# An HGRN2 / gated-MLP step on one core: how the first stage interleaves the f and q products of head 0

## The chip, the core and the metric

The kernel runs on one core of a Trainium2 chip. What is measured is the device time of one launch, in microseconds (us). Three runs of the kernel before took 1850.86, 1850.94 and 1852.46 us, median 1850.94.

A core has five engines that run their own instruction streams beside each other: PE (TensorE, matrix products; its weight loads are listed apart as PEld), DVE (VectorE), ACT (ScalarE), POOL (GpSimd) and SP (SyncE, which here issues the transfers). Each works its stream in order and waits on semaphores for what the others produce.

## The reference

The program is one step of a two-layer decoder trunk for 1024 prompt rows and 8 sample rows. Only its beginning matters here:

```python
h = x
hn = rmsnorm(h, norm_mix[0])                 # mean of squares over D_MODEL = 1024
proj = hn @ w_in                             # hgrn2_mixer
q, f, i, z = jnp.split(proj, [D_MODEL, 2 * D_MODEL, 2 * D_MODEL + D_INNER], axis=-1)
q = jax.nn.silu(q)                           # 8 heads of 128
logf = logaddexp(log(lbh), log1p(-lbh) + log_sigmoid(f));  k = -expm1(logf)
...
h = h + y
gate = jax.nn.sigmoid(rmsnorm(h, norm_ple[0]) @ w_ple_gate[0])
h = h + gate * (p[0] @ w_ple_proj[0])        # p: 256 columns a row
```

All is computed in fp32.

## The kernel before

**Layout.** Activations lie transposed: 128 partitions hold 128 features, the rows of the batch run along the columns. The 1032 rows are cut into three chunks of 384, 384 and 264 columns (`W`), and 1024 features are eight tiles, k = 0 to 7 (`KT`).

**A product in three parts.** An fp32 product is made of three passes: `mm3` (L228 to L230) multiplies high part by high part (L228), the low part of the activation by the high part of the weight (L229), and the high part of the activation by the low part of the weight (L230). A high part is a rounded copy made by ACT; a low part is what is left, a subtraction. For weights the pair is `whi` (ACT, L149) and `wlo` (DVE, L150), 128x1024 at a time; for activations it is made by `split` (L222 to L224): `bh` by ACT, `bl` by the engine handed in. One `ps_proj` tile of an output block takes 8 x 3 products.

**Who sets the order.** PE's stream is in the order of the code (a manual schedule). On the other engines a list scheduler orders instructions by priority: code position, moved forward by `tc.high_priority(offset=PRI)`; `tc.issue_after(x)` puts an instruction behind another. The code is written as generators that `Ticks` advances: a process that yields n goes on n ticks later. So tables of small numbers say how many ticks lie between the steps of a norm, and with them where a norm's two pieces of PE work stand in PE's stream: `SQD` (ticks ahead of a chunk's squares), and `SDEL[c]` (ticks from the squares to the sum, and from the sum to the broadcast).

**The first stage, in order.** Twelve products of zeros warm PE up (L113 to L118). The weights of the first p projection are loaded (`load(0)`), then p of chunks 0 and 1 (`load_p`), then x. `pple` (L339) makes twelve blocks of p's products, four for each chunk, and stores them for later. Beside them run three processes `first_norm(c)` (L579). Each squares its chunk's eight tiles on ACT and adds them in pairs (chunk 0 on DVE, the others on POOL), so four tiles remain. `norm_sum` (L266) sums over features with one-column products on PE (`pss`, L279) and raises to -1/2 on POOL; `norm_bc` (L285) broadcasts the result to all partitions by products with the identity (`pbc`, L290). Then `norm_proc` (L293) scales tile by tile on DVE (`xs`, L303, in place) and splits: `bh` on ACT (L223), `bl` on POOL for even tiles and on DVE for odd ones (L224). The same `norm_proc` serves the two later norms that precede the per-layer gate.

Then come head 0's products, chunk by chunk: `fk` (L600) makes f with 24 products, reads the sum with two sigmoids and two scalings on ACT (L606 to L609); `qq` (L614) makes q with 24 more, one sigmoid and a multiplication on DVE (L620). The f weight is `take("a", 8)`, the q weight `take("a", 0)`; `take` also starts the split of the next weight in line. The norm of a later chunk runs while the products of the chunk ahead of it run, and its sum and broadcast stand between them: chunk 1's both inside chunk 0's products, chunk 2's broadcast between f and q of chunk 1. After chunk 2's q the z products of head 0 follow (two blocks m over three chunks), and beside them `mix_x` forms sums and differences of the normed x on DVE (L426 to L429) for the rest of z.

## Time and profile before

| | |
|---|---|
| three runs, median (lowest to highest) | 1850.94 us (1850.86 to 1852.46) |
| the profiled execution's own time | 1854.45 us |
| its span (first to last instruction) | 1852.4 us |
| busy in the span: PE / DVE / ACT / POOL | 1817.2 / 1364.2 / 896.1 / 403.7 us |
| instructions of PE / DVE / ACT / POOL | 14458 / 2760 / 1905 / 407 |

The profile is of one execution, 3.5 us longer than the median of the three runs. A row of the timeline reads: start, length, engine, line, operation, output<-inputs with their shapes, how many such instructions in a row stand in this row (x4), and in brackets the engine's idle time ahead of it with what ended it. A row with a count gives the time from the start of its first instruction to the end of its last. Durations overlap where an engine pipelines, so the spacing of starts is the cost of one in a row of many.

The table by stretches gives, for each stretch of the span, its length and, for PE, PEld, DVE, ACT and POOL in that order, the busy time and the number of instructions, then the granted TensorE clock (1.00 is full), and the DMA engines' share and rate. Lines of the kind `PE out L229 <- DVE bl L224: a, n, b` are waits: an engine and line, what it waited for, the total wait, how many, and the longest.

### The profile page before, as it was taken

How to read it: one execution, taken by the hardware profiler on the slowest of the kernel's cores; microseconds unless marked ns; L12 is line 12 of the kernel's file. 1: busy time of each engine (PE TensorE's matmuls, PEld its weight loads, DVE VectorE, ACT ScalarE, POOL GpSimd, SP SyncE). 2: the span in 40 equal slices, each digit the busy share in tenths (PEclk: the TensorE clock that was granted, in tenths of full speed). 3: DMA queues.
4: the chain of work that ended last, by engine and by line, in shares of the span. 5: the costliest groups of instructions: out<-in, count | busy, mean ns of one | idle time of the engine just before them, and what ended most of it. 6: DMA issues, size and time to landing. Idle time of an engine off the chain costs nothing.

```text
span 1852.4 us, 37136 instructions
## 1 busy us (share of the span) xinstructions
PE 1817.2 (98%) x14458; PEld 1784.3 (96%) x14458; DVE 1364.2 (74%) x2760; ACT 896.1 (48%) x1905; POOL 403.7 (22%) x407
## 2 busy tenths in 40 slices
PE   8999999999999999999999999999999999999997
PEld 7999999999999999999999999999999998999997
DVE  7766788889788886877746755577778877877744
ACT  7533366556656656454435544433343345445442
POOL 4000011111011110000324233354444551000222
PEclk9999999999999999999999999999999999999999
DMA  6233343346444357863144433323334546953223
GB/s 222 79 111 104 116 128 119 118 142 190 143 136 135 113 170 223 273 206 105 57 163 137 123 106 91 102 84 124 123 101 148 177 124 223 295 190 98 69 92 115
DMA packets 164561, 258.11 MB, mean 139 GB/s; under 512 B 16097, under 2 KB 136865, under 8 KB 163361
## 3 DMA queue, kind: packets, MB, share of 16 engines
q1 hardware_dynamic: 164384, 255.74, 43.6%
q8 instruction: 113, 1.85, 0.4%
q14 instruction: 64, 0.52, 0.1%
HBM read 182.88 MB, written 72.80 MB: 138 GB/s over the span
## 4 chain that ended last, share of the span: by engine, by line
PE 81%; DVE 10%; DMA 5%; issue 2%; POOL 1%; ACT 1%; SPq 0%; DVEq 0%; POOLq 0%; ACTq 0%
PE ps_proj L228 19%; PE ps_proj L230 19%; PE ps_proj L229 19%; PE ps_d L228 3%; PE ps_d L230 3%; PE ps_d L229 3%; PE ps_o L228 2%; PE ps_o L230 2%; PE ps_o L229 2%; DMA vb<-vd 1%; PE psp L1528 1%; DVE wlo L150 1%; PE pt_o L901 1%; PE pt_g L1410 1%; DVE bl L224 1%
## 5 line engine op out<-in xcount | busy, mean ns | idle before, releaser
L228 PE MATMUL ps_proj<-bh,whi 128*128 128x264 f32 (+1 forms) x2248 | 719.3, 320 | 4.8 <-ACT u L494 1.6
L229 PE MATMUL ps_proj<-bl,whi 128*128 128x264 f32 (+1 forms) x2248 | 700.9, 312 | 5.3 <-DVE bl L224 2.7
L230 PE MATMUL ps_proj<-bh,wlo 128*128 128x264 f32 (+1 forms) x2248 | 700.9, 312 | 1.2 <-DVE wlo L150 1.2
L228 PEld LDWEIGHTS ps_proj<-bh,whi 128*128 128x128 f32 x2248 | 423.4, 188 | 12.8 <-PE pt_k L873 3.5
L229 PEld LDWEIGHTS ps_proj<-bl,whi 128*128 128x128 f32 x2248 | 423.9, 189 | 8.8 <-DVE bl L224 5.5
L230 PEld LDWEIGHTS ps_proj<-bh,wlo 128*128 128x128 f32 x2248 | 422.4, 188 | 2.1 <-DVE wlo L150 2.1
L150 DVE TENSOR_TENSOR wlo<-wstg,whi 128x1024 fp32r<-128x1024 f32 x148 | 186.7, 1261 | 110.1 <-ACT whi L149 109.8
L149 ACT CAST whi<-wstg 128x1024 fp32r<-128x1024 f32 x148 | 155.3, 1049 | 147.5 <-PE ps_proj L229 124.6
L149 ACT CAST shi<-ssum 128x512 fp32r<-128x512 f32 x152 | 94.0, 622 | 190.3 <-PE ps_proj L229 90.7
L150 DVE TENSOR_TENSOR slo<-ssum,shi 128x512 fp32r<-128x512 f32 x152 | 113.7, 751 | 9.4 <-ACT shi L149 8.9
L237 POOL TENSOR_TENSOR rsq<-rms_e,mhalf 128x3 f32<-128x3 f32 x15 | 17.8, 1187 | 359.7 <-DVE rms_e L282 359.7
L859 DVE TENSOR_TENSOR qk<-qk,t 128x384 f32<-128x384 f32 (+1 forms) x144 | 77.4, 541 | 11.9 <-PE pC L809 11.1
L228 PE MATMUL ps_proj<-xmh,shi 128*128 128x384 f32 x244 | 83.1, 340 | 0.5 <-DVE u L498 0.3
L230 PE MATMUL ps_proj<-xmh,slo 128*128 128x384 f32 x244 | 81.8, 335 | 0.0
L229 PE MATMUL ps_proj<-xml,shi 128*128 128x384 f32 x244 | 81.7, 335 | 0.0
L228 PE MATMUL ps_o<-bh,whi 128*128 128x384 f32 (+1 forms) x232 | 73.5, 317 | 0.0
L230 PE MATMUL ps_o<-bh,wlo 128*128 128x384 f32 (+1 forms) x232 | 72.8, 314 | 0.0
L229 PE MATMUL ps_o<-bl,whi 128*128 128x384 f32 (+1 forms) x232 | 72.7, 314 | 0.0
L1537 POOL TENSOR_TENSOR s<-s,u 128x384 f32<-128x384 f32 (+1 forms) x48 | 54.1, 1127 | 71.2 <-DVE s L1531 70.6
L1276 DVE TENSOR_TENSOR tmp<-tmp,pj 128x384 f32<-128x384 f32 (+1 forms) x48 | 25.6, 534 | 55.9 <-ACT tmp L1275 52.1
L237 POOL TENSOR_TENSOR rsq<-ss_e,mhalf 128x3 f32<-128x3 f32 (+2 forms) x32 | 28.7, 896 | 143.2 <-DVE ss_e L895 143.2
L264 POOL TENSOR_TENSOR ssq<-ssq,tmp 128x384 f32<-128x384 f32 (+1 forms) x36 | 34.2, 951 | 108.0 <-ACT tmp L263 108.0
(376 smaller groups left out, 4134.1 us busy)
## 6 DMA issues: line engine op xcount, KB each, us to landing
wstg<-in_wina SPq DMA_DIRECT2D x48, 512.0 KB, 3.7
wstg<-in_winb SPq DMA_DIRECT2D x48, 512.0 KB, 4.2
pj<-ppd SPq DMA_DIRECT2D x16, 516.0 KB, 4.5
S<-in_st SPq DMA_DIRECT2D x16, 512.0 KB, 5.6
vb<-vd SPq DMA_DIRECT2D x16, 512.0 KB, 4.9
out_so_s<-S SPq DMA_DIRECT2D x16, 512.0 KB, 3.5
wstg<-in_wouta SPq DMA_DIRECT2D x16, 512.0 KB, 4.1
wstg<-in_wgate SPq DMA_DIRECT2D x16, 512.0 KB, 3.7
```

Of the source, the lines that this page charges most:

```text
L149: A.copy(hi, src)
L150: V.tensor_tensor(lo, src, hi.bitcast(F32), ALU.subtract)
L224: last["lo"] = eng.tensor_tensor(lo, src, hi.bitcast(F32), ALU.subtract)
L228: PE.matmul(ps, wh, xh, start=first, stop=False, skip_group_check=more)
L229: PE.matmul(ps, wh, xl, start=False, stop=False, skip_group_check=more)
L230: PE.matmul(ps, wl, xh, start=False, stop=last, skip_group_check=more)
L237: G.tensor_tensor(y, e, mhalf[:, :n], ALU.pow)
L264: eng.tensor_tensor(ssq, ssq, sq[:, :w], ALU.add)
L859: V.tensor_tensor(lev, lev, t2.rearrange("p two (n o) -> p two n o", o=1).broadcast_to([P, 2, n, lv]), ALU.mult)
L901: PE.transpose(pt[:, m, :], on[:, m * P:(m + 1) * P], ident)
L1276: V.tensor_tensor(gt[:, :w], gt[:, :w], pj[:, OFF[c]:OFF[c] + w], ALU.mult)
L1537: G.tensor_tensor(s[:, :w], s[:, :w], us[mm, c][:, :w], ALU.mult)
```

## The change

It edits the code of the first stage and the functions that this stage calls (`load_p`, `pple`, `norm_proc`).

- **Warm-up.** The zeros are 128 columns wide; each of the twelve products reads one of them, broadcast to 512 columns.
- **Loads.** The first weight goes, as two pieces of 256 and 768 columns, through `load_split` into tiles that belong to chunk 2's activations (`hh[2]`, `hl[2]`, free so early). The transfers are issued as: first piece, p of chunk 0 (two halves, by `load_p(..., single=True)`), second piece, p of chunk 1, x of chunk 0. Two further weights are fetched ahead of x of chunk 1. Chunk 0's p is split in two halves, the weight in two pieces.
- **Order on PE.** `proj2` makes f and q of chunks 0 and 1 together: three products for f, then three for q, for each k, with a tick behind each of the first six. Chunk 2 has f, then q, as before. So there are more ticks in a chunk, and `SQD` and `SDEL` have other numbers.
- **Norms.** In the first norms all low parts are made by DVE, the scaling of tile j waits in the order until the low part of tile j-2 has been issued, and both have a raised priority. In chunks 1 and 2 the squares are not added in pairs, so `norm_sum` sums eight tiles instead of four.
- **ACT.** The copies that read out the first half of p's products have a raised priority. A sigmoid of a scrap tile (`gone`) follows the preparation of lb, which brings the table load forward; the squares of chunk 2 stand behind the last split of chunk 1, not its fourth.
- **Later norms.** `norm_proc` sets `high_priority(offset=0)` around the scaling and the split of every other norm. There nothing is raised, but the instructions of DVE and ACT come out in another order.

The diff, cut to its core:

```diff
-SQD = (0, 6, 12)
+SQD = (0, 11, 17)
 KB = 1
-SDEL = ((6, 3), (6, 2), (4, 2))
+SDEL = ((8, 2), (7, 2), (8, 2))
...
-        zf = zp.tile([P, 512], F32, name="zf")
+        zf = zp.tile([P, P], F32, name="zf")
         V.memset(zf, 0.0)
-        zr = zp.tile([P, 512], F32R, name="zr")
+        zr = zp.tile([P, P], F32R, name="zr")
         V.tensor_copy(zr, zf)
         zo = zps.tile([P, 512], F32, name="zo")
         for _ in range(NWARM):
-            PE.matmul(zo, zr[:, :P], zr, start=True, stop=True)
+            PE.matmul(zo, zr, zr[:, 0:1].broadcast_to([P, 512]), start=True, stop=True)
...
+        lows = []
         for j in range(KT):
             t = src(j) if own else sp.tile([P, 384], F32, name="tmp", bufs=4)
-            V.scalar_tensor_tensor(t[:, :w], src(j), g32[:, gi, j:j + 1], pbc[:, :w], ALU.mult, ALU.mult)
-            split(hh[:, j, :], hl[:, j, :], t[:, :w], V if j % 2 else G)
+            with tc.high_priority(offset=PRI if own else 0):
+                with tc.issue_after(lows[j - 2].ins) if own and j > 1 else ExitStack():
+                    V.scalar_tensor_tensor(t[:, :w], src(j), g32[:, gi, j:j + 1], pbc[:, :w], ALU.mult, ALU.mult)
+                split(hh[:, j, :], hl[:, j, :], t[:, :w], V if j % 2 or own else G)
+            lows.append(last["lo"])
...
-    def load_p(ap, l, c, ph, pl, behind=None, to=None):
+    def load_p(ap, l, c, ph, pl, behind=None, to=None, single=False):
         stg = ap.tile([P, 2, W[c]], F32, name=f"pstg{c}", bufs=1)
+        if single:
+            ph[c], pl[c] = [ap.tile([P, 2, W[c]], F32R, name=f"p{x}{c}") for x in "hl"]
+            for k in range(2):
+                load_split(ph[c][:, k], pl[c][:, k], pT[l][:, k, OFF[c]:OFF[c] + W[c]], stg[:, k])
+            return
...
-                with tc.high_priority(offset=PRI if l else 0):
+                with tc.high_priority(offset=0 if half and not l else PRI):
...
-    load(0)
+    loaded[0] = [t.rearrange("p k t -> p (k t)")[:, :1024] for t in (hh[2], hl[2])]
+    w0stg = wp.tile([P, 1024], F32, name="wstg")
+
+    def first_weights(a, b):
+        load_split(loaded[0][0][:, a:b], loaded[0][1][:, a:b], wproj[0, 0][:, a:b], w0stg[:, a:b])
+
     ph, pl = [None] * 3, [None] * 3
-    load_p(sp, 0, 0, ph, pl)
+    first_weights(0, 2 * P)
+    load_p(sp, 0, 0, ph, pl, single=True)
+    first_weights(2 * P, 1024)
     load_p(sp, 0, 1, ph, pl)
...
+    fetch_weights(1)
+    fetch_weights(2)
     load_x(1)
-    fetch_weights(1)
     load_x(2)
-    fetch_weights(2)
...
-        eng = V if c == 0 else G
         for j in range(0, KT, 2):
 
-            with tc.issue_after(last["pple" if c == 1 else "split4"].ins) if c else ExitStack():
+            with tc.issue_after(last["pple" if c == 1 else "split"].ins) if c else ExitStack():
                 A.activation(sq[:, j:j + 2, :], xs[c][:, j:j + 2, :], AF.Square)
-            eng.tensor_tensor(sq[:, j, :], sq[:, j, :], sq[:, j + 1, :], ALU.add)
-        yield from norm_proc(sp, [sq[:, j, :] for j in range(0, KT, 2)], lambda j: xs[c][:, j, :], 0, hh[c], hl[c], c, SDEL[c], True)
+        yield from norm_proc(sp, [sq[:, j, :] for j in range(0, KT, 1 if c else 2)], lambda j: xs[c][:, j, :], 0, hh[c], hl[c], c, SDEL[c], True)
...
+    gone = sp.tile([P, NH], F32, name="gone")
...
+    A.activation(gone, lb[:, 3, :], AF.Sigmoid)
+
+    def proj2(w1, w2, c):
+
+        both = [(wt, pp.tile([P, 512], F32, name="ps_proj", tag="mm", bufs=3)) for wt in (w1, w2)]
+        for k in range(KT):
+            for (wh, wl), ps in both:
+                mm3(ps[:, :W[c]], blk(wh, k), blk(wl, k), hh[c][:, k, :], hl[c][:, k, :], k == 0, k == KT - 1)
+            if k < KT - 2:
+                tk.tick()
+        return [ps for _, ps in both]
...
-        if i == 8:
-            with tc.issue_after(last["pple"].ins):
-                load(1)
+        if i == 5:
+            load(2)
         tk.tick()
     r0 = new_head()
-    wf, wq = take("a", 8), take("a", 0)
+    wf, wq = take("a", 8), loaded[2]
     for c in CH:
-        fk(0, r0, wf, c)
-        qq(0, r0, wq, c)
+        pf, pq = proj2(wf, wq, c) if c < 2 else (None, None)
+        fk(0, r0, wf, c, pf)
+        if c == 2:
+            take("a", 0)
+        qq(0, r0, wq, c, pq)
```

Three places show what that makes of the streams. In the names a number behind the underscore tells buffers apart; "x2" is two alike in a row.

The first is PE's stream at chunk 2's broadcast (`pbc`). Before, it stood between f and q of chunk 1: ahead of it products with the f weight (`whi_218`), behind it 24 products of the same chunk (`bh1`) with the q weight (`whi_494`).

```order
L228 MATMUL ps_proj_644<-bh1_137,whi_218 128x384
L229 MATMUL ps_proj_644<-bl1_140,whi_218 128x384
L230 MATMUL ps_proj_644<-bh1_137,wlo_219 128x384
L290 MATMUL pbc_675<-ident_68,rsq3_642 128x128 x2
L290 MATMUL pbc_675<-ident_68,rsq3_642 128x8
L228 MATMUL ps_proj_703<-bh1_137,whi_494 128x384
L229 MATMUL ps_proj_703<-bl1_140,whi_494 128x384
L230 MATMUL ps_proj_703<-bh1_137,wlo_495 128x384
```

Now f (`whi_224`) and q (`whi_288`) of chunk 1 alternate ahead of it, and behind it come at once the products of chunk 2 (`bh2`, `bl2`), which are made from this broadcast.

```order
L228 MATMUL ps_proj_631<-bh1_137,whi_224 128x384
L229 MATMUL ps_proj_631<-bl1_140,whi_224 128x384
L230 MATMUL ps_proj_631<-bh1_137,wlo_225 128x384
L228 MATMUL ps_proj_632<-bh1_137,whi_288 128x384
L229 MATMUL ps_proj_632<-bl1_140,whi_288 128x384
L230 MATMUL ps_proj_632<-bh1_137,wlo_289 128x384
L290 MATMUL pbc_788<-ident_68,rsq3_762 128x128 x2
L290 MATMUL pbc_788<-ident_68,rsq3_762 128x8
L228 MATMUL ps_proj_819<-bh2_138,whi_224 128x264
L229 MATMUL ps_proj_819<-bl2_141,whi_224 128x264
L230 MATMUL ps_proj_819<-bh2_138,wlo_225 128x264
```

So the 24 products of q that lay between the broadcast and the first product that needs it lie there no more.

The second place is DVE's stream behind chunk 0's broadcast. Before, five scalings came first, then the f weight's low part, and DVE's four low parts lay among the rest; the other four were POOL's.

```order
L303 SCALAR_TENSOR_TENSOR xs0_154<-xs0_154,g32_72,pbc_374 128x384 x5
L150 TENSOR_TENSOR wlo_219<-wstg_194,whi_218 128x1024
L282 TENSOR_SCALAR rms_e_481<-pss_432 128x3
L224 TENSOR_TENSOR bl0_139<-xs0_154,bh0_136 128x384 x2
L303 SCALAR_TENSOR_TENSOR xs0_154<-xs0_154,g32_72,pbc_374 128x384 x3
L224 TENSOR_TENSOR bl0_139<-xs0_154,bh0_136 128x384 x2
L150 TENSOR_TENSOR wlo_495<-wstg_200,whi_494 128x1024
```

Now scalings and low parts alternate, all eight of each on DVE, and the low parts of both weights (`wlo_225` of f, `wlo_289` of q) stand among them.

```order
L306 SCALAR_TENSOR_TENSOR xs0_154<-xs0_154,g32_72,pbc_385 128x384 x2
L150 TENSOR_TENSOR wlo_225<-wstg_194,whi_224 128x1024
L224 TENSOR_TENSOR bl0_139<-xs0_154,bh0_136 128x384
L306 SCALAR_TENSOR_TENSOR xs0_154<-xs0_154,g32_72,pbc_385 128x384
L224 TENSOR_TENSOR bl0_139<-xs0_154,bh0_136 128x384
L306 SCALAR_TENSOR_TENSOR xs0_154<-xs0_154,g32_72,pbc_385 128x384
L150 TENSOR_TENSOR wlo_289<-wstg_196,whi_288 128x1024
L224 TENSOR_TENSOR bl0_139<-xs0_154,bh0_136 128x384
L306 SCALAR_TENSOR_TENSOR xs0_154<-xs0_154,g32_72,pbc_385 128x384
L224 TENSOR_TENSOR bl0_139<-xs0_154,bh0_136 128x384
```

DVE's first low part moved from behind seven instructions to behind three, the q weight's from the end of the chunk to its middle.

The third place is DVE's stream behind chunk 2's broadcast, after the change alone (before, five scalings of 264 columns stood in a row, and POOL made half of the low parts). L648 is chunk 1's multiplication for q.

```order
L306 SCALAR_TENSOR_TENSOR xs2_156<-xs2_156,g32_72,pbc_788 128x264 x2
L648 TENSOR_TENSOR qk_783<-ps_proj_632,sg_816 128x384
L224 TENSOR_TENSOR bl2_141<-xs2_156,bh2_138 128x264
L306 SCALAR_TENSOR_TENSOR xs2_156<-xs2_156,g32_72,pbc_788 128x264
L224 TENSOR_TENSOR bl2_141<-xs2_156,bh2_138 128x264
L306 SCALAR_TENSOR_TENSOR xs2_156<-xs2_156,g32_72,pbc_788 128x264
L224 TENSOR_TENSOR bl2_141<-xs2_156,bh2_138 128x264
```

The pairs go on like this to the eighth low part, ahead of which stands one of the sums for z (L438). So each low part but the last stands behind one more scaling than the low part ahead of it, and the multiplication ahead of them all.

More of the change, by code (lines that the diff above doesn't have):

```diff
@@ L582, in first_norm @@
         sq = sp.tile([P, KT, 384], F32, name="sq0", bufs=2)[:, :, :W[c]]
-        eng = V if c == 0 else G
         for j in range(0, KT, 2):
-            with tc.issue_after(last["pple" if c == 1 else "split4"].ins) if c else ExitStack():
+            with tc.issue_after(last["pple" if c == 1 else "split"].ins) if c else ExitStack():
                 A.activation(sq[:, j:j + 2, :], xs[c][:, j:j + 2, :], AF.Square)
-            eng.tensor_tensor(sq[:, j, :], sq[:, j, :], sq[:, j + 1, :], ALU.add)
-        yield from norm_proc(sp, [sq[:, j, :] for j in range(0, KT, 2)], lambda j: xs[c][:, j, :], 0, hh[c], hl[c], c, SDEL[c], True)
+            if not c:
+                V.tensor_tensor(sq[:, j, :], sq[:, j, :], sq[:, j + 1, :], ALU.add)
+        yield from norm_proc(sp, [sq[:, j, :] for j in range(0, KT, 1 if c else 2)], lambda j: xs[c][:, j, :], 0, hh[c], hl[c], c, SDEL[c], True)
+    gone = sp.tile([P, NH], F32, name="gone")
     V.tensor_tensor(lb[:, 1, :], lb[:, 0, :], lb[:, 0, :], ALU.subtract)
@@ L597, in trunk_kernel, with fk @@
     V.tensor_scalar(lb[:, 3, :], lb[:, 2, :], -1.0, 1.0, ALU.mult, ALU.add)
-    def fk(h, r, wt, c):
+    A.activation(gone, lb[:, 3, :], AF.Sigmoid)
[7 more added lines that the diff above has]
+        return [ps for _, ps in both]
+    def fk(h, r, wt, c, ps=None):
         w = W[c]
-        ps = proj(wt, hh[c], hl[c], c)
+        ps = ps or proj(wt, hh[c], hl[c], c)
         f = fq.tile([P, 384], F32, name="f", bufs=3)
@@ L612, in fk, with qq @@
         tk.tick()
-    def qq(h, r, wt, c):
+    def qq(h, r, wt, c, ps=None):
         w = W[c]
-        ps = proj(wt, hh[c], hl[c], c)
+        ps = ps or proj(wt, hh[c], hl[c], c)
         sg = fq.tile([P, 384], F32, name="sg", bufs=2)
```

## The prediction

> **What bounds the kernel now.** I read the page first, then busy time by stretch, then who waited for whom on TensorE (PE), and last the timeline of PE, VectorE (DVE) and ScalarE (ACT) in the first 60 us. On the page:
>
> ```profile
> PE 81%; DVE 10%; DMA 5%; issue 2%; POOL 1%; ACT 1%; SPq 0%; DVEq 0%; POOLq 0%; ACTq 0%
> ```
>
> PE carries 81% of the chain that ends last, so an edit counts by what it does to PE's start, PE's work and PE's waits. The change edits what runs before about 59 us, so the stretches that matter are these (start:end, length, then busy time and count of PE, PEld, DVE, ACT, POOL, then clock, DMA):
>
> ```profile
> 7.30:20.97 13.67, 13.67 (x175) 12.63 (x173) 7.45 (x18) 12.60 (x23) 5.30 (x6) 1.00 1.08 372
> 20.97:36.64 15.67, 12.57 (x247) 10.56 (x247) 14.72 (x22) 11.36 (x23) 10.72 (x10) 1.00 0.69 223
> 36.64:47.96 11.32, 9.97 (x63) 8.99 (x55) 10.28 (x21) 6.34 (x16) 6.55 (x7) 1.00 0.01 3
> 47.96:54.31 6.35, 6.06 (x49) 5.84 (x49) 6.35 (x14) 5.13 (x12) 1.12 (x2) 1.00 0.00 0
> 54.31:58.96 4.65, 4.46 (x26) 4.14 (x25) 4.65 (x9) 4.65 (x11) 0.00 (x0) 1.00 0.53 130
> 58.96:1852.40 1793.44, 1765.14 (x13901) 1738.01 (x13900) 1318.09 (x2678) 852.90 (x1821) 379.79 (x380) 1.00 0.44 138
> ```
>
> They are: A the products of p; B, C, D head 0's f and q on chunks 0, 1, 2; E the first z product. PE waits in B and C, mostly for the low parts:
>
> ```profile
> PE ps_proj L229 <- POOL bl L224: 2.4, 3, 1.1
> PE ps_proj L229 <- DVE bl L224: 2.0, 3, 1.1
> PE ps_proj L230 <- DVE wlo L150: 0.3, 1, 0.3
> ```
>
> **Prices.** All are spacings, start to start, since the durations overlap.
>
> ```profile
> 8.31 0.34 PE L228 MATMUL ps_pple<-ph,whi 128*128 128x384 f32 x1
> 9.35 0.34 PE L228 MATMUL ps_pple<-ph,whi 128*128 128x384 f32 x1
> 14.20 0.98 PE L279 MATMUL pss<-ones,sq 128*32 128x1 f32 x96
> 15.11 0.44 PE L228 MATMUL ps_pple<-ph,whi 128*128 128x384 f32 x1
> 57.31 2.88 DVE L224 TENSOR_TENSOR xzl<-xs,xzh 128x384 fp32r<-128x384 f32 x6
> 31.65 2.19 DVE L303 SCALAR_TENSOR_TENSOR xs<-xs,g,pbc 128x384 f32<-128x384 f32 x4 [0.82 <-PE pbc L290]
> 21.53 1.22 DVE L150 TENSOR_TENSOR wlo<-wstg,whi 128x1024 fp32r<-128x1024 f32 x1
> 43.94 2.08 DVE L303 SCALAR_TENSOR_TENSOR xs<-xs,g,pbc 128x264 f32<-128x264 f32 x5
> 48.75 0.42 DVE L224 TENSOR_TENSOR bl<-xs,bh 128x264 fp32r<-128x264 f32 x1
> 49.09 1.11 DVE L427 TENSOR_TENSOR xs<-xs 128x384 f32<-128x384 f32 x1
> ```
>
> Six 384-column products in 1.04 us: 0.173 each; 264 columns: 24 in 2.9 us of D's 6.35 (two sets and 0.55 of waits), 0.12 each. A norm's sum (96 records) holds PE for 0.91. On DVE with POOL idle, a 384 low part is (2.88-0.55)/5 = 0.47; a scaling (L303) of 384 is 0.53, of 264 0.40; a 264 low part 0.34; a weight's low part 1.22.
>
> **A, the start (-1.05 us).**
>
> ```profile
> 1.01 0.48 DVE L113 MEMSET zf<- 128x512 f32 x1
> 1.53 0.43 DVE L115 CAST zr<-zf 128x512 fp32r<-128x512 f32 x1
> 2.01 5.49 PE L118 MATMUL zo<-zr 128*128 128x512 f32 x12 [2.01 <-DVE zr L115]
> 4.57 1.05 ACT L149 CAST whi<-wstg 128x1024 fp32r<-128x1024 f32 x1 [2.49 <-DMA wstg<-in_wproj]
> 7.30 0.52 PE L228 MATMUL ps_pple<-ph,whi 128*128 128x384 f32 x1
> 7.80 0.50 PE L229 MATMUL ps_pple<-pl,whi 128*128 128x384 f32 x1
> 8.13 0.34 PE L230 MATMUL ps_pple<-ph,wlo 128*128 128x384 f32 x1
> ```
>
> The zeros shrink to a quarter of the columns, so 0.9 us of DVE becomes about 0.3 and the warm-up starts near 1.4. It lasts 5.29 (2.01 to 7.30), so p's products start near 6.7. Their data is there: the first 512 KB landed by 4.57, the first three loads now carry those bytes, and behind them stand three small casts (0.41, 0.41, 0.28 by the rates above) and DVE's 0.41: about 6.2. The late pl at 7.80 and a wait at 14.20 go too (0.45). Two table-free copies and the two added load issues lie beside PE. 0.6 + 0.45 = 1.05. PE is at half rate up to 8.13 (0.33 between the last two rows, 0.17 after), 6.1 us after the warm-up's start; I let that move with the start.
>
> [...]
>
> **B, chunk 0 (-1.4).** Behind the broadcast (now ending near 18.5, two products before A's end at 19.9), DVE does two scalings, the f weight's low part and the first low part: 1.06+1.14+0.55 and two hand-overs, 21.3. PE's second product waits from 19.9+0.2: 1.3. Then DVE does scaling, low part, scaling, q weight's low part (0.53+0.47+0.53+1.22), so q's third product waits to 24.0: 1.9 more. From there DVE needs 0.53+0.47 = 1.00 per k and PE 6 x 0.173 = 1.04: no wait. B ends at 24.0 + 43 x 0.173 + 0.2 (restarts) + 1.82 + 0.75 = 34.2, where 1.82 is the sum of chunk 1, whose eight squares are no longer added in pairs (192 records), and 0.75 the broadcast. Length 14.3 against 15.67. POOL's 10.72 us of B are gone, and with them DVE's slow spells.
>
> **C, chunk 1 (+1.8).** The broadcast now stands directly ahead of the products that need it. ACT has chunk 0's reads first:
>
> ```profile
> 33.36 1.28 ACT L606 ACT_TABLE_LOAD   x1
> 34.65 0.49 ACT L606 ACTIVATE f<-ps_proj 128x384 f32<-128x384 f32 x1
> 43.32 0.49 ACT L606 ACTIVATE f<-ps_proj 128x384 f32<-128x384 f32 x1 [3.86 <-PE ps_proj L230]
> 43.71 0.49 ACT L607 ACTIVATE qk<-ps_proj 128x384 f32<-128x384 f32 x1
> 44.08 0.71 ACT L608 ACTIVATE f<-f,lb 128x384 f32<-128x384 f32 x1
> 44.68 0.61 ACT L609 ACTIVATE qk<-qk,lb 128x384 f32<-128x384 f32 x1
> 45.19 1.66 ACT L223 CAST bh<-xs 128x264 fp32r<-128x264 f32 x5
> ```
>
> Three sigmoids of 0.38, 0.60 and 0.51 are 2.25, from 33.1 (f ends 0.5 before q): 35.4. Cast and low part end at 36.5, 2.3 after the broadcast. PE does one product in that time; 47 follow: 36.5 + 8.1 + 0.1 + 1.82 + 0.73 = 47.3. C is 13.1 against 11.32. The table load moves to about 15 us, where ACT has slack; cost nothing.
>
> [...]
>
> **D, chunk 2 (+4.05).** Before, this broadcast stood ahead of chunk 1's q, whose 24 products hid most of DVE's chain:
>
> ```profile
> 43.12 0.73 PE L290 MATMUL pbc<-ident,rsq 128*128 128x128 f32 x6
> 43.71 0.42 PE L228 MATMUL ps_proj<-bh,whi 128*128 128x384 f32 x1
> 51.06 0.39 PE L229 MATMUL ps_proj<-bl,whi 128*128 128x264 f32 x1 [0.29 <-DVE bl L224]
> 52.17 1.06 ACT L149 CAST whi<-wstg 128x1024 fp32r<-128x1024 f32 x1
> 55.01 0.45 PE L230 MATMUL ps_proj<-bh,wlo 128*128 128x384 f32 x1 [0.19 <-DVE wlo L150]
> ```
>
> 43.85 to 51.06 is 7.2 us for that chain. Now f alone follows, three products (0.36) per k, while DVE takes 0.40+0.34 = 0.74. From 47.3: two scalings 0.80, q's multiplication 0.46 (it stands ahead of the first low part), 0.34, then 7 x 0.74 and one mixing instruction 0.47: 54.6 with hand-overs. PE ends f at 54.9 and q, 2.9 later, at 57.8. D is 10.4 against 6.35.
>
> **E, the z weights (+0.7).** They reuse f's buffer, so their cast waits for f's end as at 52.17. ACT now has one cast and four activations ahead (0.4, then 0.28+0.28+0.50+0.40), cast 1.05, low part 1.22: 59.1, when PE has waited since 58.1; with the restarts 5.35 against 4.65.
>
> **Other edits.** The later norms' DVE instructions stand in another order. PE's wait there before was
>
> ```profile
> PE ps_proj L229 <- DVE bl L224: 0.3, 1, 0.3
> ```
>
> in each of two places. The second low part comes some 4 us later, just when PE needs it, the last one at about the same time: between -0.3 and +1 each. I take 0, since the last one ends the wait. PE's order after E is unchanged.
>
> **Sum.** -1.05 - 1.4 + 1.8 + 4.05 + 0.7 = +4.1 us, on a profiled execution of 1854.45 (span 1852.4): 1858.5 with a profile like it. It ran 3.5 above the runs' median, 1850.94, so the forecast is **1855.0**, +0.22%. About 0.2%, 3.7 us, is what a measurement of this kernel can tell from no change.
>
> **Rivals.**
> - Not slower: D's chain doesn't hold PE. At up to 0.62 us per k instead of 0.74, D loses 0.9 less, and with C's wait near 1.5 the sum is +2.3; at PE's own 0.36 it is about +1.1 (1852.0). It turns below 3.7 us once a pair costs under 0.69. For it: the 264 rows were read while POOL was still at work. Against it: those six 384 low parts with POOL idle show the same rate per column.
> - Faster: the waits of B to E go altogether, and only PE's work stays: A -1.05, B 10.9, C 10.9, D 5.8, E 4.15: -7.3, 1843.6. It needs every first low part ready as PE arrives; the order of DVE speaks against it.
> [...]
> - The clock drops in D, where PE works under half the time for 7 us. At half rate, as up to 8.13, q of chunk 2 costs 2.9 more: +7.0, 1858. Against it: B ran with 3.1 us of waits at clock 1.00. [...]
>
> That the low parts don't go to DVE is no rival: POOL's queue has none left in this stage.
>
> **How the numbers follow.** Forecast 0.64, own range +2.0 to +6.0: 0.40 above 3.7 us, 0.24 under. Not slower 0.12 and earlier clock 0.06, both within 0.2%; faster 0.08; clock drop 0.10, slower. Together: slower 0.50, same 0.42, faster 0.08. The range, 1850.5 to 1858.5, leaves out the faster case and the tail of the last. [...]
>
> **What would show it.** A: first p product near 6.7. B: one wait for bl, one for the q weight's wlo, then none. C: a wait of about 2 behind the broadcast, and 192 sum records. D: eight waits for bl, 0.74 apart, q's end near 57.8. E: a wait for wlo near 1 us. It is wrong if f of chunk 2 ends before 53, or if z's first product comes before 56.

## The result, and the profile after

The changed kernel took 1866.28 us (median of six runs, 1864.32 to 1869.69), the kernel before 1852.70 on the same chip (six runs, 1850.86 to 1856.01). The ratio is 1.0072, interval 1.0061 to 1.0082: **13.6 us slower**, outside the range on record. The profiled execution ran 1865.37 us, its span is 1863.7, so it shows 11.3 of the 13.6 us.

The same stretches of the changed kernel as were shown of before, in the view by stretches: first product of p to f's first (A), chunk 0 (B), chunk 1 (C), chunk 2 (D), the first z block on chunk 0 (E), the rest.

```profile
5.90:20.68 14.78, 13.73 (x175) 12.61 (x173) 7.53 (x17) 12.96 (x24) 0.86 (x1) 1.00 1.05 361
20.68:34.78 14.10, 11.69 (x246) 10.73 (x246) 8.93 (x17) 9.93 (x20) 0.86 (x1) 1.00 0.85 272
34.78:50.78 16.00, 13.20 (x247) 12.42 (x246) 12.57 (x27) 6.39 (x14) 1.09 (x1) 0.89 0.01 3
50.78:61.10 10.32, 8.63 (x49) 7.67 (x49) 10.28 (x26) 7.51 (x18) 0.00 (x0) 0.83 0.00 0
61.10:66.19 5.09, 4.43 (x26) 4.12 (x25) 5.09 (x9) 5.09 (x13) 0.00 (x0) 1.00 0.45 146
66.19:1863.70 1797.51, 1768.19 (x13901) 1740.22 (x13900) 1314.74 (x2675) 856.36 (x1821) 379.89 (x380) 1.00 0.43 137
```

Two things stand out beside the lengths. The clock column, 1.00 throughout before, reads 0.89 in C and 0.83 in D. And the rest, where PE's order is unchanged, is 4.1 us longer than the 1793.44 before.

| | forecast | measured |
|---|---|---|
| start and A (to f's first product) | -1.05 | -0.29 |
| B | -1.4 | -1.57 |
| C | +1.8 | +4.68 |
| D | +4.05 | +3.97 |
| E | +0.7 | +0.44 |
| the rest | 0 | +4.07 |
| sum | +4.1 | +11.3 |

PE's waits in the first 62 us (engine and line, waited for, total, times, longest):

```profile
PE ps_proj L228 <- ACT bh L223: 3.0, 3, 1.7
PE ps_proj L230 <- DVE wlo L150: 1.7, 1, 1.7
PE ps_proj L229 <- DVE bl L224: 1.2, 3, 0.7
PE pss L279 <- issue: 1.0, 1, 1.0
```

The first three are the waits that were foreseen: behind the broadcasts, for the q weight's low part, for the first low parts. The fourth is new. It stands in C, in PE's timeline:

```profile
42.40 1.38 PE L279 MATMUL pss<-ones,sq 128*32 128x1 f32 x144
44.74 0.57 PE L279 MATMUL pss<-ones,sq 128*32 128x1 f32 x48 [0.96 <-issue]
...
45.70 0.34 PE L230 MATMUL ps_proj<-bh,wlo 128*128 128x384 f32 x1
45.88 0.38 PE L228 MATMUL ps_proj<-bh,whi 128*128 128x384 f32 x1
46.06 0.52 PE L229 MATMUL ps_proj<-bl,whi 128*128 128x384 f32 x1
46.38 0.52 PE L230 MATMUL ps_proj<-bh,wlo 128*128 128x384 f32 x1
```

PE stops for 0.96 us inside chunk 2's sum and waits for nothing that the profile shows. No data can be missing: the records go column by column, 64 to each, and the first 64 have read all eight tiles already. Behind the sum the products' spacing goes from 0.18 to 0.32 us, and it is back at 0.18 by 49.5. The view by stretches of 3.41 us shows the clock there:

```profile
42.62:46.03 3.41, 2.45 (x192) 2.34 (x181) 2.02 (x7) 0.51 (x1) 0.34 (x1) 1.00 0.03 7
46.03:49.44 3.41, 3.41 (x13) 3.41 (x12) 2.85 (x7) 0.00 (x0) 0.75 (x1) 0.50 0.00 0
49.44:52.86 3.42, 2.02 (x14) 1.72 (x13) 2.04 (x6) 2.97 (x7) 0.00 (x0) 1.00 0.00 0
52.86:56.27 3.41, 3.41 (x15) 3.10 (x14) 3.41 (x11) 1.99 (x5) 0.00 (x0) 0.50 0.00 0
```

From 46.03 to 49.44 and from 52.86 to 56.27 the clock is 0.50. Each time the stretch of the same length ahead holds one-column sums, the broadcast or waits, and few products. The chunk 1 sum, at 30.11, has 192 records too and doesn't stop.

### The profile page after: what moved, and what is told of

It is laid out like the page before. It is cut to its first block, busy times and chain, and to the rows that moved or that the text cites. A ratio compares the mean times of both kernels' runs of the same rounds, so it can differ in the third digit from the quotient of the medians.

```text
span 1863.7 us, 37507 instructions
## 1 busy us (share of the span) xinstructions
PE 1824.4 (98%) x14650; PEld 1791.4 (96%) x14650; DVE 1361.0 (73%) x2774; ACT 900.9 (48%) x1908; POOL 382.9 (21%) x387
## 4 chain that ended last, share of the span: by engine, by line
PE 79%; DVE 11%; DMA 4%; issue 2%; ACT 1%; POOL 1%; SPq 0%; DVEq 0%; ACTq 0%; POOLq 0%
PE ps_proj L228 19%; PE ps_proj L230 18%; PE ps_proj L229 18%; PE ps_d L228 3%; PE ps_d L230 3%; PE ps_d L229 3%; PE ps_o L228 2%; PE ps_o L229 2%; PE ps_o L230 2%; DVE wlo L150 1%; DVE bl L224 1%; PE psp L1558 1%; DVE qk L889 1%; DMA zstg<-ozd 1%; PE pt_g L1440 1%
## 5 line engine op out<-in xcount | busy, mean ns | idle before, releaser
L889 DVE TENSOR_TENSOR qk<-qk,t 128x384 f32<-128x384 f32 (+1 forms) x144 | 77.6, 543 | 11.4 <-PE pC L839 10.5
L1567 POOL TENSOR_TENSOR s<-s,u 128x384 f32<-128x384 f32 (+1 forms) x48 | 54.7, 1142 | 66.9 <-DVE s L1561 66.3
L1306 DVE TENSOR_TENSOR tmp<-tmp,pj 128x384 f32<-128x384 f32 (+1 forms) x48 | 26.1, 548 | 56.0 <-ACT tmp L1305 49.5
```

The costliest lines, as they stand in the source:

```text
L889: V.tensor_tensor(lev, lev, t2.rearrange("p two (n o) -> p two n o", o=1).broadcast_to([P, 2, n, lv]), ALU.mult)
L1306: V.tensor_tensor(gt[:, :w], gt[:, :w], pj[:, OFF[c]:OFF[c] + w], ALU.mult)
L1567: G.tensor_tensor(s[:, :w], s[:, :w], us[mm, c][:, :w], ALU.mult)
```

## The experiments

Every kernel ran five times or more beside the kernel before on the same chip, whose median lay between 1855.1 and 1856.4. "z" is the time at which the z products begin in the profile (before 54.3, changed 61.1). The third column is the difference of the two medians; the ratio is estimated from all runs of both kernels, so the two can differ by about 1 us. Where two rows of the table are set against each other below, the intervals of both leave an uncertainty of 2 to 3 us.

| run | median us | against before | ratio, interval | z |
|---|---|---|---|---|
| again (changed, unaltered) | 1868.94 | +13.6 | 1.0069, 1.0057 to 1.0081 | 63.7 |
| pairs_back | 1863.79 | +7.4 | 1.0044, 1.0032 to 1.0056 | 60.4 |
| early_broadcast | 1867.12 | +10.8 | 1.0061, 1.0048 to 1.0073 | 60.5 |
| old_norm_order | 1865.37 | +10.1 | 1.0052, 1.0039 to 1.0065 | 60.8 |
| mended (those three) | 1858.20 | +3.0 | 1.0021, 1.0012 to 1.0030 | 58.0 |
| unpaired (on before) | 1862.46 | +6.9 | 1.0033, 1.0020 to 1.0045 | 60.4 |
| late_broadcast (on before) | 1858.14 | +2.8 | 1.0017, 1.0009 to 1.0025 | 62.3 |
| f_then_q | 1867.76 | +11.4 | 1.0065, 1.0052 to 1.0077 | 60.1 |
| keep_busy | 1871.79 | +15.4 | 1.0083, 1.0067 to 1.0098 | 66.9 |
| spread | 1864.04 | +8.7 | 1.0048, 1.0036 to 1.0060 | 63.3 |
| spread_pairs | 1856.95 | +1.4 | 1.0011, 1.0002 to 1.0020 | 57.1 |
| spread_pool | 1858.80 | +3.3 | 1.0019, 1.0011 to 1.0028 | 58.2 |
| weights_first | 1856.81 | +1.7 | 1.0014, 1.0005 to 1.0023 | 56.1 |
| busy_waits | 1857.78 | +2.7 | 1.0017, 1.0008 to 1.0026 | 56.4 |

### The doubled sums: pairs_back, unpaired

```diff
-            if not c:
-                V.tensor_tensor(sq[:, j, :], sq[:, j, :], sq[:, j + 1, :], ALU.add)
+            (G if c else V).tensor_tensor(sq[:, j, :], sq[:, j, :], sq[:, j + 1, :], ALU.add)
```

with `range(0, KT, 2)` for the tiles that are summed.

> The changed kernel, with the squares of chunks 1 and 2 added in pairs on POOL again, so that each of these sums has 96 records instead of 192. In the changed kernel chunk 1 (from the end of its broadcast's wait to chunk 2's broadcast, 34.8 to 50.8) lasted 16.0 us, PE ran at half clock from 46.0 to 49.4 and stood for 0.96 us inside the 192 records of chunk 2's sum. Theory S (the doubled sums make all that was not forecast in this chunk: 0.9 us of work, the 0.96 us stop, and a stretch that PE's clock gate takes for idle): chunk 0 lasts 13.2 instead of 14.1, chunk 1 12.5, no stop and no half clock before 50 us, and the z products start near 57 instead of 61.1; the run is 3 to 5 us shorter than the changed kernel's. Rival C (the clock's fall is a matter of where its windows lie, or of PE's waits at the broadcasts): the half clock stays, chunk 1 lasts about 15, z starts near 59; 1 to 2 us shorter.

Chunk 1 came out at the 12.5 us that theory S expects, without a stop and at clock 1.00. The rows are B, C and D of this kernel:

```profile
20.91:37.26 16.35, 13.65 (x150) 12.69 (x150) 10.60 (x17) 9.92 (x20) 9.51 (x9) 0.79 0.70 231
37.26:49.78 12.52, 10.65 (x151) 9.96 (x150) 11.92 (x26) 6.39 (x14) 1.17 (x1) 1.00 0.01 3
49.78:60.40 10.62, 8.07 (x49) 6.39 (x50) 10.46 (x27) 7.48 (x18) 0.00 (x0) 1.00 0.00 0
```

But the half clock had not gone, as rival C expects and theory S doesn't. It now lay in B (clock 0.79), which took 16.35 us instead of 14.10, so z gained only 0.7 in this profile. D took 10.6 at full clock: its 10.3 in the changed kernel was not made by the clock. The runs gained 6.2 us against the changed kernel's +13.6, with an uncertainty of about 3. The other way round, on the kernel before:

> The kernel before, with one thing of the change: the squares of chunks 1 and 2 are not added in pairs on POOL, so each of these sums has 192 records instead of 96. In seven profiles with such sums PE stops for 0.6 to 4.1 us inside them, each time while or just after 16 KB of instructions are fetched; in the two profiles with 96 records it doesn't. Theory I (so many small instructions in a row use up what PE has of its stream ahead, and it waits for the next fetch): each sum takes 0.9 us more, at least one of the two stops for 0.5 to 2.3 us with no other engine to wait for, z starts at 56 to 58.5 instead of 54.3, and the run is 1.5 to 4 us longer than the kernel before. Rival R (those stops came from the interleave's order, not from the number of records): no stop over 0.3 us; the time POOL gains pays for the sums, z starts under 55.5.

PE's timeline of that kernel around its two large sums:

```profile
21.22 1.54 PE L279 MATMUL pss<-ones,sq 128*32 128x1 f32 x164
26.91 0.59 PE L279 MATMUL pss<-ones,sq 128*32 128x1 f32 x28 [4.15 <-issue]
...
38.53 1.63 PE L279 MATMUL pss<-ones,sq 128*32 128x1 f32 x174
42.38 0.43 PE L279 MATMUL pss<-ones,sq 128*32 128x1 f32 x18 [2.22 <-issue]
```

Stops of 4.15 and 2.22 us, both in the last column of the sum. With each the clock falls to half for 6.83 us, where the kernel before had none in this stage:

```profile
24.72:31.55 6.83, 4.64 (x41) 4.62 (x41) 3.48 (x8) 2.97 (x7) 2.42 (x3) 0.50 0.78 242
41.79:48.62 6.83, 6.24 (x36) 6.22 (x36) 4.87 (x10) 0.47 (x2) 3.09 (x3) 0.50 0.01 4
```

So z, at 60.4, and the loss, 6.9 us in the runs (3.7 to 8.3 by the interval), go beyond what theory I expects (58.5 and 4). On the stops it holds and R falls: neither interleave nor new order is needed for them. What PE may be waiting for shows in the transfers of that window, on the queue that the profile calls instruction:

```profile
q8 instruction: 1, 0.02, 1.2%
```

In the changed kernel each of the 115 packets on this queue is 16384 bytes. In the trace of unpaired that one 16 KB packet goes from 24.40 to 25.52, and PE goes on at 26.91; the packet of the second stop goes from 40.03 to 41.05, PE goes on at 42.38. Eight of the profiles in the table and of the changed kernel have sums of 192 records, sixteen in all. Nine of them stop, in seven profiles, and each time PE goes on 1.3 to 1.5 us after a 16 KB packet on q8 has landed. The sums of 96 records have no such stop. Of the sums of 192 that don't stop, the changed kernel's first began 0.6 us after such a packet had landed. (The expectation counts seven profiles with stops and up to 4.1 us; there were six, since keep_busy has none, and the 4.1 are two stops of spread, 1.75 and 2.31, together.)

### The place of chunk 2's broadcast: early_broadcast, late_broadcast

```diff
-SDEL = ((8, 2), (7, 2), (8, 2))
+SDEL = ((8, 2), (7, 2), (5, 2))
```

> The changed kernel with SDEL[2] = (5, 2) instead of (8, 2): chunk 2's sum stands behind the second k of chunk 1 and its broadcast behind the fourth, so 24 products lie between the broadcast and chunk 2's first product, as before the change. Theory P (the place of the broadcast is what costs in chunk 2: 10.3 us against 6.35): DVE turns to chunk 2 when the last low part of chunk 1 is done, near 44, so chunk 2's last low part is ready near 52, the z products start near 55 instead of 61.1, and the run is 5 to 6 us shorter than the changed kernel's. Rival D (DVE's 0.74 us a pair hold PE wherever the broadcast stands, and DVE has no room ahead of the end of chunk 1): chunk 2 still lasts over 9, z starts at 59.5 or later, the gain is under 2 us.

The rows of B, C and D:

```profile
20.91:36.43 15.52, 13.11 (x246) 12.16 (x246) 8.93 (x17) 9.92 (x20) 0.86 (x1) 0.89 0.75 245
36.43:53.42 16.99, 13.11 (x248) 12.42 (x248) 13.35 (x31) 7.28 (x16) 1.16 (x1) 0.90 0.01 2
53.42:60.50 7.08, 6.59 (x49) 5.97 (x49) 6.88 (x17) 6.38 (x16) 0.00 (x0) 1.00 0.00 0
```

Chunk 2 fell from 10.3 to 7.1 us, as theory P expects. Of the 5 to 6 us that it expects of the whole, the runs show 2.8, which is not clear of noise (the ratio's interval overlaps with the changed kernel's), and z came 0.6 earlier: a stop of 2.0 us inside the sum made C longer, and half clock stood in B and C. On the kernel before, the other direction:

```diff
-SDEL = ((6, 3), (6, 2), (4, 2))
+SDEL = ((6, 3), (6, 2), (4, 4))
```

> The kernel before, with SDEL[2] = (4, 4) instead of (4, 2): chunk 2's broadcast stands directly ahead of chunk 2's f, as in the changed kernel. All else is as before (low parts on POOL and DVE, f then q). Theory P (the broadcast's place is what makes chunk 2 dear): chunk 2, from the broadcast's end to the z products, lasts 9 to 10.5 us instead of 6.35, chunk 1 is at most 1 shorter, and z starts at 57 to 58.5 instead of 54.3. Rival L (it is the low parts on DVE): with POOL's help chunk 2 stays under 8, z starts under 56.

Chunk 2 took 9.99 us (before 6.35), with POOL's help for the low parts; the runs lost 2.8, clear of noise. Its profile is of the slowest of twelve runs and has 10.2 us at half clock ahead of z, hence z at 62.3. For the length of chunk 2 theory P holds on both sides; in the runs it is shown on this side alone.

### The later norms: old_norm_order

```diff
-            with tc.high_priority(offset=PRI if own else 0):
+            with tc.high_priority(offset=PRI) if own else ExitStack():
```

> The changed kernel with the raised priority only around the scalings and splits of the first norms, so that the later norms' instructions are ordered as before the change. In five profiles with the new order PE waits 1.1 us at 937 for the low part of the first weight of layer 1 (before: no wait there), and the stretch from 895 to 940 is 1.9 us longer than before. Theory N (the new order in the later norms costs this): the stretch is as long as before within 0.3 us, the 1.1 us wait goes, and the run is about 2 us shorter than the changed kernel's. Rival O (those 2 us come with the later arrival of transfers, since all before it has moved): the wait stays and the time is the changed kernel's.

In the changed kernel's timeline of PE stands

```profile
937.72 0.45 PE L230 MATMUL ps_proj<-bh,wlo 128*128 128x384 f32 x1 [1.13 <-DVE wlo L150]
```

and in this kernel's waits between 880 and 1010 us stand only

```profile
PE ps_pple L228 <- ACT pple_t L359: 0.5, 1, 0.5
PE ps_proj L229 <- DVE bl L224: 0.4, 1, 0.4
```

The 1.1 us wait is gone, and set against the same products of before the stretch is no longer (1.9 us longer in the changed kernel). The second such norm costs too. In the changed kernel PE's waits between 1735 and 1795 us are

```profile
PE ps_proj L229 <- DVE bl L224: 0.9, 2, 0.5
PE ps_proj L230 <- DVE wlo L150: 0.3, 1, 0.3
```

where the kernel before has one of 0.3 us, and the same products take 1.0 us longer; in old_norm_order they don't. Theory N holds, at 2.9 us for both norms in the trace. The runs gained 3.5, with an uncertainty of about 3 on either side.

### The clock: again, keep_busy, weights_first, busy_waits

> The changed kernel, not altered. In its first profile PE's clock stood at half from 46.0 to 49.4, from 52.9 to 56.3 and from 226.9 to 230.4; in three variants it stood at half for 3.4 or 6.8 us from about 24 on instead. Theory G (the clock is decided anew every 3.413 us, on a grid that isn't tied to the program, and a stretch of the grid in which PE's products stream for less than about a quarter of the time brings half clock in the next): the stretches at half clock lie elsewhere this time unless the grid happens to lie the same, each directly behind a 3.413 us stretch with one of the waits at the start of chunk 0, of chunk 1, of chunk 2 or at 223, and they add up to 3.4 to 10.2 us before 300; z starts between 59 and 63. Rival F (each fall belongs to a place in the program): half clock at 46.0 and 52.9 again, z at 61.1.

The stretches of the second profile of the same kernel:

```profile
21.88:25.29 3.41, 1.73 (x9) 1.41 (x9) 3.41 (x7) 3.32 (x6) 0.00 (x0) 0.99 1.07 371
25.29:28.70 3.41, 3.41 (x13) 3.41 (x12) 3.41 (x7) 1.95 (x4) 0.00 (x0) 0.51 1.07 331
35.53:38.94 3.41, 1.57 (x10) 1.12 (x9) 2.62 (x6) 2.88 (x7) 0.00 (x0) 0.99 0.00 0
38.94:42.35 3.41, 3.41 (x13) 3.41 (x12) 3.41 (x8) 1.86 (x4) 0.00 (x0) 0.51 0.00 0
```

Two more follow from 49.2 and 56.0: four stretches at half clock where the first profile had two, and at other places. Rival F falls. In theory G the grid holds: each is 3.41 us long and stands directly behind a stretch with a wait, three of them at the start of a chunk, that of 49.2 inside chunk 2's sum. Its "about a quarter" doesn't hold. The 1.73 us of PE work ahead of 25.29 cost the clock, while the same 1.73 us in the first profile did not:

```profile
22.14:25.55 3.41, 1.73 (x10) 1.40 (x10) 3.41 (x7) 3.30 (x7) 0.00 (x0) 1.00 1.06 367
25.55:28.96 3.41, 3.41 (x21) 3.41 (x20) 3.34 (x7) 1.98 (x5) 0.00 (x0) 1.00 1.07 314
```

In all, 13.7 us at half clock and z at 63.7, above what was expected.

keep_busy fills with zeros the places ahead of the two falls of the first profile:

```diff
+            if own and c == 2 and i == 2:
+                filler(6)
...
         pbc = norm_bc(rs, c)
+        if own and c == 2:
+            filler(6)
```

> The changed kernel with 6 products of zeros (512 columns, 0.2 us each) between the second and the third column of chunk 2's sum, and 6 behind its broadcast, where PE waits. Nothing else is changed. Theory S (PE's clock falls to half at 46.0 and 52.9 because the 3.4 us ahead of each hold little but one-column products and waits): the clock stays at 1.00 from 5 to 60 us; chunk 1 loses 1.6 us of slow products and gains 1.2 of zeros, so it lasts 15.6 instead of 16.0; chunk 2 keeps its 10.3, since DVE sets its pace at 0.74 us per k whatever PE's clock is; z starts at 60.5 to 61. Rival C (the fall doesn't hang on what PE does there): both stretches at 0.5 stay, chunk 1 lasts 17.2. Rival W (chunk 2 is slow because of the clock): it shortens to 8.5.

C and D ran at clock 1.00, C in 14.94 us and D in 10.64, so D again was no matter of the clock and rival W falls. Its chunk 2 sum, with six products of zeros ahead of the last column, has no stop. The time of the whole run shows nothing: with the fillers the list scheduler put the q weight's low part behind chunk 0's pairs on DVE, and PE waited 6.3 us for it.

weights_first and busy_waits are built on mended (below) and leave that order alone.

```diff
-        with tc.high_priority(offset=PRI if order[n][:2] == ("p", 1) or order[n][0] in ("b", "g") else 0):
+        with tc.high_priority(offset=PRI if n == 2 or order[n][:2] == ("p", 1) or order[n][0] in ("b", "g") else 0):
```

> The kernel called mended, with the split of the q weight at a raised priority, so that DVE makes the low parts of both weights ahead of chunk 0's first low part: PE waits there once, about 1.9 us, instead of twice (0.7 and 2.0). It is the comparison for busy_waits. Theories H (half clock behind the waits costs what is left) and D (DVE's chain costs it) both expect about what mended gave: z at 57 to 59, one or two stretches of 3.4 or 6.8 us at half clock, the run 2 to 4 us longer than the kernel before.

Two stretches of 3.41 us at half clock, as expected; z, at 56.1, and the runs, at +1.7, are a little better than expected. busy_waits adds `filler(9)` behind the first product of chunk 0 and `filler(7)` behind chunk 1's broadcast.

> Weights_first with products of zeros (512 columns, 0.215 us each) in the two places where PE waits most: 9 behind chunk 0's first product, 7 behind chunk 1's broadcast. They last 1.9 and 1.5 us, about as long as the waits, and nothing else is altered but some sums for z on DVE and copies on ACT that come in another order. Theory H (PE's clock falls because these waits leave too little in a 3.41 us stretch, and 6.8 us at half clock cost up to 3.4 us): no half clock from 20 to 50 us, z starts 2 to 3.4 us earlier than in weights_first, and the run is 2 to 3 us shorter than it, which is that of the kernel before or up to 1 us better. Rival D (DVE's pairs set the pace, so PE's clock matters little): z and the run as in weights_first within 1 us, whatever the clock does.

No half clock was left before the tail, and nothing was gained: z at 56.35 against 56.05, the runs at +2.7 against +1.7. In place of the half clock stands another wait, ahead of chunk 2's broadcast:

```profile
34.20 1.77 PE L269 MATMUL fill<-zr 128*128 128x512 f32 x7
...
44.28 0.83 PE L295 MATMUL pbc<-ident,rsq 128*128 128x128 f32 x6 [1.94 <-POOL rsq L237]
```

The sum's result goes through DVE, which is still at chunk 1's pairs. Theory H falls and D holds: with these three parts undone, DVE's chain is what PE follows, and a PE at half clock merely arrives later where it would have waited.

### The three together: mended

The diffs of pairs_back, early_broadcast and old_norm_order in one kernel.

> The changed kernel with three of its parts undone together: the squares of chunks 1 and 2 added in pairs on POOL again (sums of 96 records), chunk 2's broadcast four k ahead of the end of chunk 1 (SDEL[2] = (5, 2)), the later norms in their old order. The interleave, the low parts on DVE and the order of loads stay. Theory M (those three are the loss, and the interleave is neither gain nor loss by itself): no stop inside the sums, chunk 1 lasts 12 to 13 us (16.0 in the changed kernel), chunk 2 6 to 7.5 (10.3), the stretch at 895 to 940 as before, z starts at 53.5 to 56.5 with 0 to 6.8 us at half clock, and the run is within 2.5 us of the kernel before on either side. Rival W (the waits of the interleave at the start of each chunk, and the half clock behind them, are a loss of their own): z at 57.5 or later, the run at least 3 us longer than the kernel before.

No stop; C 15.35 us, with 6.8 us of half clock in it, where 12 to 13 were expected, and D 7.10. Of the 13.6 us 10.6 are gone, and the three parts by themselves gave 6.2, 2.8 and 3.5, 12.5 in all: they are most of the loss. But z lay at 58.0 and the runs at +3.0, on rival W's side. weights_first, which is this kernel with one priority raised, gained nothing when busy_waits took its half clock away, which points to DVE's chain in front of each chunk for what is left. For mended itself that is argued, not shown.

### f, then q: f_then_q, spread, spread_pairs, spread_pool

f_then_q takes the interleave out of the changed kernel (`SQD = (0, 6, 12)`, `SDEL = ((8, 2), (6, 2), (4, 2))`, `proj2` not called).

> The changed kernel without the interleave: f, then q, for all three chunks, and the broadcasts and sums where they stood before (SQD (0, 6, 12), SDEL (8,2), (6,2), (4,2)); low parts on DVE, the sums of 192 records and the order of loads stay as changed. Theory P (the interleave and the broadcasts' place are the loss, the other parts are not): DVE sets the pace of f with 1.0 us a k in chunks 0 and 1 and q hides what follows; chunk 0 ends near 34, chunk 1 near 45, z starts at 50 to 52, before the 54.3 of the kernel before; the run is 8 to 10 us shorter than the changed kernel's. Rival L (the low parts on DVE are the loss): each f waits for DVE's pairs, q hides nothing more, z starts at 57 or later, and the gain is under 4 us.

It tested less than it should: chunk 1's sum now stood ahead of chunk 0's f, and PE's waits begin with

```profile
PE pss L279 <- ACT sq L602: 3.9, 4, 1.9
PE pss L279 <- issue: 2.4, 1, 2.4
```

so f started at 27.5 instead of 20.7; the stop of 2.4 us is in chunk 2's sum. From there to z it took 32.7 us against 40.4, which speaks for theory P, but the run shows no gain over 3 us. Three further versions keep f and q apart and put the sums and broadcasts better.

```diff
-SQD = (0, 11, 17)
+SQD = (0, 11, 13)
-SDEL = ((8, 2), (7, 2), (8, 2))
+SDEL = ((8, 2), (2, 1), (4, 1))
-        if i == 5:
-            load(2)
```

> A version put together from what was seen: the changed kernel with f, then q, in all chunks; chunk 1's sum behind the fourth k of chunk 0's f and its broadcast behind that f, so that q hides DVE's chain (SQD (0, 11, 13), SDEL (8,2), (2,1), (4,1)); the later norms in their old order; the q weight not fetched ahead. Low parts on DVE and the sums of 192 records stay. Theory P: PE follows DVE at 1.0 us a k in each f and isn't held in q, chunk 0 starts near 20.8, f of chunk 0 ends near 30.5, of chunk 1 near 40.5, of chunk 2 near 48, z starts at 50 to 52, no stretch at half clock but by chance, and the run is 2 to 4 us shorter than the kernel before. Rival L (low parts on DVE cost more than the place of the broadcasts): z starts at 55 or later and the run isn't shorter than the kernel before.

The times are rival L's (z at 63.3, +8.7), but not for its reason alone: PE stopped 4.1 us inside its two sums, and 17 us stood at half clock. With the pairs back:

> The version called spread (f, then q; all low parts on DVE in pairs with the scalings; later norms in their old order) with the squares of chunks 1 and 2 added in pairs on POOL, so sums of 96 records. Spread stood 4.1 us inside its sums and had 17 us at half clock, z at 63.3. Theory I: no stop inside the sums, so chunk 0 ends near 31, f of chunk 1 near 40, and z starts at 51 to 54; half clock for at most 3.4 us; the run is 0 to 3 us shorter than the kernel before. Rival L (DVE's 1.0 us a k in f alone, with PE at half its pace, is enough to lower the clock and to lose): z at 57 or later, the run at least 3 us longer than the kernel before.

z at 57.1 and +1.4 us, without a stop: between the theories, the nearest to the kernel before of all that was run, but not faster. In f of chunk 0 PE waited 2.1 us for one low part, behind the q weight's on DVE, and 10 us stood at half clock. Even tiles' low parts on POOL:

> Spread_pairs with the low parts of even tiles on POOL again, the odd ones on DVE in turn with the scalings. Theory L (low parts on DVE alone hold f to 1.0 us a k): DVE needs about 0.77 a k, POOL 1.1 to 1.5 for each second k, so f of chunks 0 and 1 are 1 to 2 us shorter each than in spread_pairs, z starts 2 to 4 us earlier. Rival M (POOL's adds and low parts slow DVE's instructions as they did in the kernel before, and the adds stand in POOL's queue ahead of low parts): no gain, z as late as in spread_pairs or later.

Rival M: z 58.2, +3.3. PE then waits for POOL's adds (1.9 us) and low parts (1.6), and still 3.3 for DVE's low parts. No version was faster than the kernel before.

## Why the prediction was wrong, step by step

- **Direction, and D.** Slower was right, and its mechanism too: chunk 2's broadcast directly ahead of its products costs DVE's chain, 3.97 us where 4.05 stood. DVE's timeline in D has the low parts 0.74 apart, as forecast:

```profile
52.10 0.43 DVE L224 TENSOR_TENSOR bl<-xs,bh 128x264 fp32r<-128x264 f32 x1
52.44 0.49 DVE L306 SCALAR_TENSOR_TENSOR xs<-xs,g,pbc 128x264 f32<-128x264 f32 x1
52.84 0.43 DVE L224 TENSOR_TENSOR bl<-xs,bh 128x264 fp32r<-128x264 f32 x1
```

  Of the eight waits for low parts PE shows two in D, since half clock stretched its products over the others: 0.22 to 0.30 us apart from 53.9 to 56.2, and 0.12 from 58.1 on. In the runs the place is worth 2.8 us (late_broadcast).
- **The step that failed first: the doubled sums.** B and C price them "1.82 ... whose eight squares are no longer added in pairs (192 records)", that is 0.9 us of PE more for each, by the record's price in the sum of 96. The work was as priced (1.78 us in B). But PE stopped inside such sums, in chunk 2's for 0.96 us here and up to 4.15 elsewhere, and half clock followed where one-column work and a stop filled much of the 3.41 us ahead: put alone into the kernel before, they brought 13.7 us of it (unpaired). That the sums are the only cause of half clock is not so: with the pairs back 6.8 us of it stood elsewhere. C came out 2.9 us above its forecast, 0.96 by the stop and 1.6 by the clock. Priced at 1.8 for both, the sums are worth 6.2 and 6.9 us in the runs (pairs_back, unpaired), each uncertain by 2 to 3.
- **The clock.** The rival priced a fall in D alone, at 0.10, and held against it that B ran with 3.1 us of waits at clock 1.00. From 10 to 62 us the clock fell in every profile but those of the kernel before and of busy_waits, and PE was at work for 1.57 to 2.45 of the 3.41 us ahead of four falls shown above. In C it costs 1.6 us: eleven products at 0.32 us instead of 0.173. In D it costs nothing, since DVE sets the pace: at clock 0.83 D took 10.3 us, at clock 1.00 10.6 in pairs_back and in keep_busy.
- **The step that failed next: "I take 0" for the later norms**, within -0.3 to +1 for each of two. The first cost 1.9 us in the trace and the second 1.0. In the first, the low part that came late was not that of an activation, which the step looked at, but that of layer 1's first weight.
- **A.** The start came at 5.90, earlier than 6.7, with the products 0.17 to 0.18 us apart from the first on (before, 0.33 up to 8.13), so the earlier clock that the chances hold at 0.06 came true; what it is worth by itself no run shows. But only 0.29 was left of 1.05: "their data is there" failed for the second piece of the weights.

```profile
6.70 0.83 ACT L223 CAST bh<-wstg 128x768 fp32r<-128x768 f32 x1 [1.56 <-DMA wstg<-in_wproj]
...
7.59 0.44 PE L228 MATMUL ps_pple<-ph,bh 128*128 128x384 f32 x1 [0.48 <-ACT bh L223]
...
8.58 0.44 PE L230 MATMUL ps_pple<-ph,bl 128*128 128x384 f32 x1 [0.37 <-DVE bl L224]
```

  It lands behind both halves of p, and PE waits twice.
- **B and E** came out as forecast (-1.57 and +0.44), B with waits of 0.7 and 1.7 us where 1.3 and 1.9 were priced. B's gain is not safe: where the half clock fell into it, it took 15.2 to 16.4 us.
- **The rest.** Of its 4.1 us, 2.9 are the two later norms. A half-clock stretch at 227 us costs about 1.6, set against the same products of before. The remaining -0.4 is the difference of gains and losses at many places, and single runs of the kernel before differ by up to 6 us.

C's 2.9, the rest's 4.1 and A's 0.8, less 0.5 by B, D and E, are the 7.2 us by which the profile lies above the sum of the prediction. That the runs lost 2.3 us more than the profiles show is no step of the kernel: the profiled execution of the kernel before ran 1.8 above the median of its six runs, that of the changed kernel 0.9 below.

The section on the change places the squares of chunk 2 behind the last split of chunk 1; it is that of chunk 0.

## What to carry to other kernels

A step that trades a few vector additions for many tiny matrix products should not be priced by the record: look in the trace for stops inside such a run (0.6 to 4.15 us here) and at the granted clock around them (0.50 for 6.83 us with each of unpaired's two). Where DVE fed PE tile by tile, what counted here was how much PE work lay between a broadcast and its first use: chunk 2 took 6.35 us with 24 products between them, 9.99 with none (late_broadcast, at clock 0.83). Where two products are interleaved, the broadcast has to move forward with them: four k earlier, chunk 2 took 7.1 us instead of 10.3. No run here changed the interleave and nothing else, so what it is worth by itself stays open. A priority guard that raises nothing (offset 0) still reorders what a list scheduler makes of everything inside it, far from the change: read the order there too.

## What the runs showed of the hardware

- PE stopped inside runs of tiny products with no data missing, by the author's reading for want of its own instructions. In nine of sixteen sums of 192 one-column records it stopped for 0.6 to 4.15 us, always in the last third, and went on 1.3 to 1.5 us after a 16 KB packet on the instruction queue had landed. That it is the fetch is read from these times; no run changed the fetch alone.
- In the stretches shown the clock fell to 0.50 for 3.41 us or twice that. Within an execution the falls lay whole stretches of 3.41 us apart: two between 46.03 and 52.86 in the first profile of the changed kernel; four, three and two between 25.29, 38.94, 49.18 and 56.01 in the second. The places differed from one to the other, so the same kernel shows half clock for 6.8 or for 13.7 us in its first 60 us. In the four stretches ahead of a fall that are shown PE was at work for 1.57 to 2.45 of the 3.41 us. What brings a fall stays open: 1.73 us of work brought one in one stretch and none in another.
- Half clock cost time here only where PE set the pace: 1.6 us in the changed kernel's C, nothing in its D. With it gone from 20 to 50 us (busy_waits), z came no earlier: 56.35 against 56.05.
